# A Hymba layer on one core: last down-projection chunk reads pre-split operands, and orders change on DVE, GpSimd and in LayerNorm

## The chip, the cores and the metric

One core of a Trainium2 chip runs the whole layer. The metric is the device time of one execution in microseconds (us). The kernel before was run three times; the profile is of one more execution.

## The reference, cut to what matters

```python
h = layer_norm(x)                                   # 2048 tokens x 1024, float32
z = h @ w_in
y = concat(s5(z...), gla(z...), rg_lru(z...))       # three mixers
mix = y @ w_out                                     # 1024 x 1024
h = layer_norm(alpha * h + mix)                     # LN1
ff = square(relu(h @ mlp_w1)) @ mlp_w2              # 1024 -> 4096 -> 1024
h = layer_norm(alpha * h + ff)                      # LN2, the output
```

All is float32. The change touches the output projection with LN1, the two products of the MLP, and LN2.

## The kernel before, in words

**Number format.** A float32 product is made of three matmuls in a reduced format (`mm3`, L226 to L228): each operand is split into a high part (an ACT copy, L1373) and a low part (a subtraction on DVE of two tiles in SBUF); the matmuls take high x high, high x low and low x high. Names in the trace are those of tiles; L75 stands for every operation of DVE or GpSimd (POOL), since a helper records them, and L82 for every DMA, all issued from SP's queue.

**Winograd form.** Both MLP products use the seven-product form of a 2x2 block product (Strassen-Winograd). Operands are sums and differences of blocks; results come from sums of the products p1 to p7. The order of the products is p1, p2, p7, p6, p3 of the group before, p4, p5. Three kinds of PSUM banks hold them: bank a (3 buffers) p1, p6, p5, p3 added up; bank b (2) p2; bank c (2) p7 and p4. Each product is evacuated one slot after it is computed.

**Stages.** (1) Up to about 672 us: input projection and mixers. (2) 672 to 846: output projection. For each of 16 row tiles of 128 tokens the sum alpha*h + mix stays in SBUF (`acc`); LN1 runs on it (`ln1_work`, L1291, one generator that takes the rows one after another); `tj_work` (L1308) then takes two rows, transposes four 128x128 blocks at a time on TensorE (L1320, into `tjp`), copies them by ACT (L1324, L1325) into `tjo` and forms the Winograd sums there with two DVE and two POOL operations; a DMA stores them to `rop_d`. `tjo` has two buffers. (3) 846 to 958: the last of that work (`tail`) beside the first products of the MLP. The left operands of the up-projection are read back from `rop_d` into `ring` tiles and split (`ring_load`, `ring_split`); operand 6, which only p3 uses, comes last. (4) To 1541: 32 steps (`Step`), 16 column blocks for each half of the tokens, 84 matmuls each (19.0 us). A step splits its weight operands `w1o`; `Step.evac` and `hsum` make the hidden blocks c11, c21, c12, c22 (squared ReLU included) and their sums s1 to s4 in `cp` tiles, and `keep` stores the seven that the next product needs to `hid_d`, 256 KB each. (5) To 1594: entry into the down-projection. The first chunk of `mlp_w2` (tile `w`) is loaded, summed on POOL and split. (6) 1594 to 2103: chunks of the down-projection (`Chunk`), two column blocks of the hidden layer each, with 8 groups (`Part`, 42 matmuls, 9.5 us) per chunk. A part loads its operands `ho_m` from `hid_d` in 8 DMAs, splits them (three splits of 128x512, one of 128x256), and `Part.evac` adds seven products into `accq` (the rows of the output), some on DVE straight from PSUM, some on POOL from ACT's copies `p_m`, `u_m`. (7) From 2103: the eighth and last chunk. Here each group's two row tiles are final after it, and LN2 follows: `Acc.ln` (L1736: statistics on DVE, a power on POOL, a last operation on DVE) and `ln_apply` (L1754: ACT scales and shifts, L1756; DVE multiplies by the gain, 128x1024; POOL and DVE add the bias, 128x512 each; two stores).

**What sets the order.** Each engine works through its instructions in program order. `run` goes through the products; a table filled by `task(n, fn)` says which other work is written at which slot (one slot per product), so the numbers in those calls are the order of DVE, ACT, POOL and SP around the products:

```python
for g in range(8):
    n = M0 + 7 * (56 + g)
    for i, k in ((0, 13), (1, 14)):
        task(n + k, acc[g].ln, i)
        task(n + k + 2 + i, acc[g].ln_apply, i)
```

Of the kernel before, what the change touches and what calls it, by code (L numbers as in the profile page):

```python
# [40 lines left out]
def hymba_layer_kernel(  # L41
# [87 lines left out]
    hid_d = dram.tile([2, 16, 7, P, BLK], F32, name="hid_d")  # L129

# [1137 lines left out]
    def out_tile(i, dh):  # L1268
# [10 lines left out]
        def ev():  # L1279
            r = accs[i][:, dh * BLK:dh * BLK + BLK]  # L1280
            V.scalar_tensor_tensor(r, r, ALPHA, box["ps"], op0=ALU.mult, op1=ALU.add)
            if dh:
                z["acc", i] = True
# [4 lines left out]
    def ln1_work():  # L1288
        for i in range(NT):
            while ("acc", i) not in z:  # L1290
                yield  # L1291
            g = ln_steps(accs[i], z["gb1"], f"ln1_{i}", 384)
            next(g)
            yield
            yield
            yield
            for _ in g:
                yield
            late.append(bind(lambda i: store(h1_d[i * P:i * P + P, :], accs[i]), i))
            yield  # L1300
            z["row", i] = True
# [6 lines left out]
    def tj_work():  # L1308
        for i in range(2 * NT):
# [3 lines left out]
            if j == 0:  # L1313
                yield
# [17 lines left out]
            if j == 3:  # L1332
                late.append(bind(z.__setitem__, ("tj", g), True))
            yield
# [79 lines left out]
    def run(groups, tasks):  # L1414
# [25 lines left out]
        for g in groups:  # L1440
            for p in ORDER:
                who = prev if p == "p3" else g
                if who is not None:
                    products(who, p)
                evac()
                if who is not None:
                    last = who, p
# [42 lines left out]
    class Step:  # L1490
# [41 lines left out]
        def keep(self, i, nm):  # L1532
            store(hid_d[self.sb, self.c, i], self.out[nm])
# [45 lines left out]

    steps = [Step(n) for n in range(32)]  # L1580
# [24 lines left out]
    def tail():  # L1605
# [9 lines left out]
        for _ in range(4):  # L1615
# [12 lines left out]
    for n in range(11):  # L1628
# [8 lines left out]
    for n in range(31):  # L1637
# [25 lines left out]
    class Chunk:  # L1663
        def __init__(self, c):
            self.c = c
            self.op = [None] * 7

        def load(self):
            self.b = {}
            for j in range(2):  # L1670
                r = raw_tile([P, 2, D], f"w2_{self.c}_{j}")
                k = 4 * self.c + 2 * j
                load(r, w2_v[:, k:k + 2, :])
                self.b.update({("11", j): r[:, 0, 0:512], ("12", j): r[:, 0, 512:D],
                               ("21", j): r[:, 1, 0:512], ("22", j): r[:, 1, 512:D]})
# [458 lines left out]
```

## Time and profile before

| what | us |
|---|---|
| three runs | 2255.2, 2258.49, 2260.07 (median 2258.49) |
| the profiled execution | 2259.39 |
| its span in the trace | 2257.7 |
| PE busy in the span | 2067.0 (92%) |
| DVE, ACT, POOL busy | 1584.5, 1027.0, 1147.3 |
| DMA | 145 GB/s over the span |

PE is TensorE's matmul stream, PEld its weight loads, DVE the vector engine, ACT the scalar engine, POOL GpSimd, SP the engine whose queue issues the DMAs. A timeline row gives start, duration, engine, line, operation and tiles, and in brackets the engine's idle time before it with what ended it. PEclk is the granted share of TensorE's clock. The execution is 1.7 us longer than the span.

### The profile page before, as it was taken

Reading aid. Unit: us, or ns where it says so; the run is one execution under the profiler, and the core shown is the slowest. Engines: PE = TensorE matmul, PEld = TensorE weight load, DVE = VectorE, ACT = ScalarE, POOL = GpSimd, SP = SyncE. Lnnn points to the kernel's source line nnn. Section 1 sums busy time; section 2 is a strip of 40 time slices with the busy share of each in tenths; the row PEclk is TensorE's granted clock in tenths of the full one; section 3 lists DMA queues with packets and bytes.
Section 4 is the critical chain, followed back from the end, with each engine's and each line's share of the span. In section 5 each row is a group of like instructions: output and inputs, shape, how many; then the busy total and the mean of one; then the engine's idle time right before and its main releaser. Section 6 shows DMA issues by size and latency. Waiting matters only on the chain. (4 is left out here: it accounts for less than half of the span.)

```text
span 2257.7 us, 29781 instructions
## 1 busy us (share of the span) xinstructions
PE 2067.0 (92%) x9920; PEld 1712.9 (76%) x9920; DVE 1584.5 (70%) x2262; ACT 1027.0 (45%) x2045; POOL 1147.3 (51%) x1087
## 2 busy tenths in 40 slices
PE   6977999899999998799999999998999999999863
PEld 6866779888987776588887888886788888888652
DVE  6567865546547556677778877776688888888887
ACT  3336655657663222333334433334544545444431
POOL 5486630000003444466666666666566675667554
PEclk9998999999999999899999999999999999999976
DMA  7342354455354676544447444437544344434332
GB/s 212 102 129 74 98 167 137 121 138 140 99 177 131 175 232 204 146 150 153 150 154 256 151 153 154 148 128 266 185 131 135 94 134 131 135 98 134 111 105 77
DMA packets 378457, 328.24 MB, mean 145 GB/s; under 512 B 72240, under 2 KB 314560, under 8 KB 378304
## 3 DMA queue, kind: packets, MB, share of 16 engines
q1 hardware_dynamic: 377536, 324.24, 46.5%
q0 software_dynamic: 768, 2.11, 0.4%
q8 instruction: 78, 1.28, 0.2%
q14 instruction: 75, 0.61, 0.1%
HBM read 208.23 MB, written 118.63 MB: 145 GB/s over the span
## 5 line engine op out<-in xcount | busy, mean ns | idle before, releaser
L75 DVE TENSOR_TENSOR ho_m<-ho_m 128x512 fp32r<-128x512 f32 (+1 forms) x256 | 259.3, 1038 | 68.2 <-ACT ho_m L1373 55.9
L75 POOL TENSOR_TENSOR accq<-accq,p_m 128x512 f32<-128x512 f32 x128 | 199.9, 1579 | 200.4 <-DVE accq L75 155.9
L75 POOL TENSOR_TENSOR cp<-cp,cp 128x512 f32<-128x512 f32 x128 | 196.0, 1540 | 183.2 <-ACT cp L1562 180.6
L75 DVE TENSOR_TENSOR w1o_s<-w_s,w1o_s 128x512 fp32r<-128x512 f32 x160 | 208.6, 1318 | 46.6 <-ACT w1o_s L1373 46.5
L75 POOL TENSOR_TENSOR ss<-ss,cst 128x4 f32<-128x4 f32 x16 | 17.6, 1102 | 365.8 <-DVE ss L75 365.8
L227 PE MATMUL pa_m<-act,ho_m 128*128 128x512 f32 x384 | 150.4, 392 | 2.0 <-DVE act L75 1.9
L226 PE MATMUL pa_m<-act,ho_m 128*128 128x512 f32 x384 | 150.3, 391 | 2.0 <-ACT p_m L1792 1.4
L228 PE MATMUL pa_m<-act,ho_m 128*128 128x512 f32 x384 | 150.1, 391 | 1.2 <-DVE ho_m L75 1.2
L1373 ACT ACTIVATE ho_m<-ho_m 128x512 fp32r<-128x512 f32 (+1 forms) x256 | 135.6, 569 | 30.7 <-DMA ho_m<-hid_d 30.7
L1373 ACT ACTIVATE w1o_s<-w_s 128x512 fp32r<-128x512 f32 x160 | 99.9, 626 | 103.1 <-PE pb_s L228 51.8
L1792 ACT ACTIVATE p_m<-pa_m 128x512 f32<-128x512 f32 x64 | 38.3, 599 | 221.7 <-PE pa_m L228 216.0
L226 PE MATMUL pa_s<-ring,w1o_s 128*128 128x512 f32 x256 | 103.0, 402 | 11.0 <-ACT ring L1373 6.3
L226 PE MATMUL pc_m<-act,ho_m 128*128 128x512 f32 x256 | 102.4, 400 | 5.5 <-ACT p_m L1792 5.4
L226 PE MATMUL po<-act,w_mx 128*128 128x512 f32 x256 | 106.9, 418 | 0.1
L75 POOL TENSOR_TENSOR accq<-accq,u_m 128x512 f32<-128x512 f32 x64 | 106.2, 1659 | 0.6 <-ACT u_m L1792 0.6
L75 DVE SCALAR_TENSOR_TENSOR cp<-cp 128x512 f32<-128x512 f32 x96 | 101.9, 1061 | 3.3
L227 PE MATMUL pa_s<-ring,w1o_s 128*128 128x512 f32 x256 | 102.2, 399 | 1.9 <-DVE ring L75 1.9
L228 PE MATMUL po<-act,w_mx 128*128 128x512 f32 x256 | 103.2, 403 | 0.9 <-DVE w_mx L75 0.9
L227 PE MATMUL pc_s<-act,w1o_s 128*128 128x512 f32 x256 | 101.4, 396 | 1.8 <-DVE act L75 1.8
L227 PE MATMUL po<-act,w_mx 128*128 128x512 f32 x256 | 102.8, 402 | 0.0
L226 PE MATMUL pc_s<-act,w1o_s 128*128 128x512 f32 x256 | 102.6, 401 | 0.0
L228 PE MATMUL pc_m<-act,ho_m 128*128 128x512 f32 x256 | 101.5, 397 | 0.5 <-DVE ho_m L75 0.5
(437 smaller groups left out, 6553.3 us busy)
## 6 DMA issues: line engine op xcount, KB each, us to landing
hid_d<-cp SPq DMA_DIRECT2D x224, 256.0 KB, 2.3
ho_m<-hid_d SPq DMA_DIRECT2D x384, 128.0 KB, 2.3
w_s<-in_mlp_w_dram SPq DMA_DIRECT2D x32, 1024.0 KB, 5.7
w<-in_mlp_w_dram SPq DMA_DIRECT2D x16, 1024.0 KB, 7.0
rop_d<-tjo SPq DMA_DIRECT2D x32, 448.0 KB, 4.6
w<-s5w_d SPq DMA_DIRECT2D x16, 640.0 KB, 5.1
xr<-in_x_dram SPq DMA_DIRECT2D x16, 512.0 KB, 4.9
h_d<-xr SPq DMA_DIRECT2D x16, 512.0 KB, 4.4
```

The costliest lines, as they stand in the source:

```text
L75: return fn(*a, **k)
L226: T.matmul(ps, lhs[0], rhs[0], start=first, stop=False, skip_group_check=more)
L227: T.matmul(ps, lhs[0], rhs[1], start=False, stop=False, skip_group_check=more)
L228: T.matmul(ps, lhs[1], rhs[0], start=False, stop=last, skip_group_check=more)
L1373: S.activation(dst_hi, src, COPY)
L1792: S.activation(t, ps, COPY)
```

## The change

1. **Last chunk.** The chunks' column blocks are drawn from a table `CHUNK`; the last chunk takes blocks 3 and 11. Steps 3, 11, 19 and 27 make these; they no longer `keep` their seven tiles (28 stores fewer) but pass each through `parts`: an ACT copy into `hx` (2 buffers), a DVE subtraction in place, two stores to `hidx_d` (28 copies, 28 subtractions, 56 stores more). In the last chunk `Part.load` reads high and low parts with 16 DMAs in place of 8, and `split` does nothing.
2. **Part.evac.** For c21 and c22 DVE's add from PSUM is written before POOL's add of `u2` or `p7`.
3. **LN2.** Row tile 1 of a group is normalised at slots 10 and 12, row tile 0 at 13 and 15.
4. **LN1.** Each row has its own generator, started when its sum is complete; `tj_work` yields once more per four transposes; the tail goes over 18 slots in place of 11, with 6 yields before operand 6 is split.
5. **p3 of step 0** is computed at p7 of step 2 (before: in step 1); step 0's sums and step 2's operand 6 follow later.
6. **First chunk.** Its two weight tiles are loaded five slots before the last step and at it, and each is summed by itself.

```diff
                 last[0].evac(last[1])
             last = None
 
-        for g in groups:
+        for at_, g in enumerate(groups):
             for p in ORDER:
-                who = prev if p == "p3" else g
-                if who is not None:
-                    products(who, p)
-                evac()
-                if who is not None:
-                    last = who, p
+                if p != "p3":
+                    who = [(g, p)]
+                    if at_ == 2 and p == "p7":
+                        who.insert(0, (groups[0], "p3"))
+                else:
+                    who = [(groups[at_ - 1], p)] if at_ > 1 else []
+                for w in who:
+                    products(*w)
+                    evac()
+                    last = w
+                if not who:
+                    evac()
                 for e in tasks.pop(n, ()):
                     e()
                 n += 1
...
         def keep(self, i, nm):
-            store(hid_d[self.sb, self.c, i], self.out[nm])
+            if self.c not in CHUNK[-1]:
+                store(hid_d[self.sb, self.c, i], self.out[nm])
+
+        def parts(self, i, nm):
+
+            hi = z["sump"].tile([P, BLK], F32R, tag="hx", name=f"hx_{self.nm}_{i}", bufs=2)
+            raw = self.out[nm]
+            split(hi, raw.bitcast(F32R), raw)
+            for j, t in enumerate((f(hi), raw)):
+                store(hidx_d[self.sb, CHUNK[-1].index(self.c), i, j], t)
...
+    CHUNK = ((0, 1), (2, 4), (5, 6), (7, 8), (9, 10), (12, 13), (14, 15), (3, 11))
...
-        for _ in range(4):
+        for _ in range(6):
             yield
         for hf in range(2):
             ring_split(0, 6, hf)
...
-    for n in range(11):
+    for n in range(18):
...
-        for i, k in ((2, 2), (3, 3), (4, 4), (5, 6), (6, 6)):
+        for i, k in ((2, 2), (3, 3), (4, 4), (5, 6), (6, 11 if n == 1 else 6)):
             task(b + max(k, o), m.split, i)
     for n in range(32):
         s = 7 * n + 7
-        for w, k in ((1, 5), (3, 6), (2, 6), (4, 7)):
+        for w, k in ((1, 10), (3, 10), (2, 11), (4, 11)) if n == 0 else ((1, 5), (3, 6), (2, 6), (4, 7)):
             task(s + k, steps[n].hsum, w)
+        if steps[n].c in CHUNK[-1]:
+            for i, nm, k in ((0, "c11", 6), (4, "c22", 7), (2, "s3", 7), (5, "s1", 8), (1, "c21", 8), (3, "s2", 9),
+                             (6, "s4", 9)):
+                task(s + k, steps[n].parts, i, nm)
...
             for j in range(2):
-                load(f(t[:, 1, :, j, :]), hid_d[sb, 2 * self.ch.c + j, ops, :, tk].rearrange("o p c -> p o c"))
+                if self.ch.c < 7:
+                    load(f(t[:, 1, :, j, :]), hid_d[sb, CHUNK[self.ch.c][j], ops, :, tk].rearrange("o p c -> p o c"))
+                    continue
+                for h in range(2):
+                    load(f(t[:, h, :, j, :]), hidx_d[sb, j, ops, h, :, tk].rearrange("o p c -> p o c"))
...
-            split(t[:, 0], t[:, 1], f(t[:, 1]))
+            if self.ch.c < 7:
+                split(t[:, 0], t[:, 1], f(t[:, 1]))
...
             elif p == "p7":
-                self.add("c22", G, self.copy(bank["c"], "p7"))
+                self.p7 = self.copy(bank["c"], "p7")
             elif p == "p6":
-                self.add("c21", G, self.copy(bank["a"], "u2"))
+                self.u2 = self.copy(bank["a"], "u2")
             elif p == "p4":
                 self.add("c21", V, bank["c"])
+                self.add("c21", G, self.u2)
             elif p == "p5":
                 self.add("c22", V, bank["a"])
+                self.add("c22", G, self.p7)
...
-    task(L0, chunks[0].load)
-    for k, w in ((2, 3), (3, 1), (4, 2), (6, 4)):
+    task(L0 - 5, chunks[0].load, 0)
+    task(L0, chunks[0].load, 1)
+    for k, w, j in ((0, 3, 0), (1, 1, 0), (2, 3, 1), (3, 1, 1)):
+        task(L0 + k, chunks[0].sum, w, (j,))
+    for k, w in ((4, 2), (6, 4)):
         task(L0 + k, chunks[0].sum, w)
...
     for g in range(8):
         n = M0 + 7 * (56 + g)
-        for i, k in ((0, 13), (1, 14)):
+        for i, k in ((1, 10), (0, 13)):
             task(n + k, acc[g].ln, i)
-            task(n + k + 2 + i, acc[g].ln_apply, i)
+            task(n + k + 2, acc[g].ln_apply, i)
```

In `ln1_work` the outer loop over the rows and the wait for the row's sum are gone, and `active.append(ln1_work(i))` stands where the sum is complete; in `tj_work` a second `yield` stands at the end of the loop, and a wait for the first of the two rows ahead.

**DVE in the last chunk, one group.** Names are tiles of group 62, with LN2 of group 61 (`accq_5`); `gb2` holds gain and bias. Before:

```order
L75 TENSOR_TENSOR accq_6_0_13577<-accq_6_0_13577,pb_m62_18683 128x512
L75 TENSOR_TENSOR ho_m62_3_18644<-ho_m62_3_18644 128x256
L75 TENSOR_TENSOR ho_m63_1_18634<-ho_m63_1_18634 128x512
L75 TENSOR_TENSOR accq_4_1_13519<-accq_4_1_13519,gb2_18163 128x1024
L75 TENSOR_TENSOR accq_4_1_13519<-accq_4_1_13519,gb2_18163 128x512
L75 TENSOR_TENSOR ho_m63_2_18654<-ho_m63_2_18654 128x512
L75 TENSOR_TENSOR accq_5_0_13542<-accq_5_0_13542,pa_m61_18558 128x512
L75 TENSOR_TENSOR accq_6_1_13578<-accq_6_1_13578,pc_m62_18700 128x512
L75 BN_STATS st2_5_0_18756<-accq_5_0_13542 128x6 x2
L75 BN_AGGR mv2_5_0_18759<-st2_5_0_18756 128x2
L75 TENSOR_SCALAR rs2_5_0_18761<-mv2_5_0_18759 128x1
L75 SCALAR_TENSOR_TENSOR rs2_5_0_18761<-mv2_5_0_18759,rs2_5_0_18761 128x1
```

After:

```order
L75 TENSOR_TENSOR accq_6_0_13689<-accq_6_0_13689,pb_m62_18810 128x512
L75 BN_STATS st2_5_1_18842<-accq_5_1_13656 128x6 x2
L75 BN_AGGR mv2_5_1_18845<-st2_5_1_18842 128x2
L75 TENSOR_SCALAR rs2_5_1_18847<-mv2_5_1_18845 128x1
L75 SCALAR_TENSOR_TENSOR rs2_5_1_18847<-mv2_5_1_18845,rs2_5_1_18847 128x1
L75 TENSOR_TENSOR accq_5_0_13655<-accq_5_0_13655,pa_m61_18693 128x512
L75 TENSOR_TENSOR accq_5_1_13656<-accq_5_1_13656,gb2_18282 128x1024
L75 TENSOR_TENSOR accq_5_1_13656<-accq_5_1_13656,gb2_18282 128x512
L75 TENSOR_TENSOR accq_6_1_13690<-accq_6_1_13690,pc_m62_18825 128x512
L75 BN_STATS st2_5_0_18885<-accq_5_0_13655 128x6 x2
L75 BN_AGGR mv2_5_0_18888<-st2_5_0_18885 128x2
L75 TENSOR_SCALAR rs2_5_0_18890<-mv2_5_0_18888 128x1
```

The splits `ho_m` are gone. The statistics of row 1 stand in the first half of the group and those of row 0 in the second, and row 1's multiplication by the gain stands between them, ahead of the add of `pc_m`.

**ACT at the passage into the MLP.** `tjo_31` is the last transposed tile, `ring_0_6` operand 6 of the left side, `w1o_s2` the weight operands of step 2, `cp<-pa_s0` the evacuation of p3 of step 0. Before:

```order
L1324 ACTIVATE tjo_31_8775<-tjp_31_8747 128x256
L1325 ACTIVATE tjo_31_8775<-tjp_31_8747 128x128
L1373 ACTIVATE w1o_s2_1_8794<-w1_s2_8686 128x512
L1373 ACTIVATE w1o_s2_2_8814<-w1_s2_8686 128x512
L1537 ACTIVATE p7_s1_8829<-pc_s1_8797 128x512
L1373 ACTIVATE ring_0_6_0_8788<-ring_0_6_0_8788 128x2x512
L1373 ACTIVATE ring_0_6_1_8789<-ring_0_6_1_8789 128x2x512
L1373 ACTIVATE w1o_s2_3_8835<-s2_s2_8792 128x512
L1537 ACTIVATE u2_s1_8850<-pa_s1_8722 128x512
L1373 ACTIVATE w1o_s2_4_8852<-w1_s2_8686 128x512
L1561 ACTIVATE cp_4_8867<-pa_s0_8485 128x512
```

After:

```order
L1324 ACTIVATE tjo_31_8820<-tjp_31_8815 128x256
L1325 ACTIVATE tjo_31_8820<-tjp_31_8815 128x128
L1374 ACTIVATE w1o_s2_4_8828<-w1_s2_8669 128x512
L1374 ACTIVATE w1o_s2_5_8868<-s1_s2_8722 128x512
L1374 ACTIVATE w1o_s3_0_8890<-w1_s3_8728 128x512
L1553 ACTIVATE p1_s2_8908<-pa_s2_8871 128x512
L1374 ACTIVATE ring_0_6_0_8848<-ring_0_6_0_8848 128x2x512
L1374 ACTIVATE ring_0_6_1_8849<-ring_0_6_1_8849 128x2x512
L1374 ACTIVATE w1o_s3_1_8916<-w1_s3_8728 128x512
L1577 ACTIVATE cp_6_8931<-pa_s0_8490 128x512
```

The split of operand 6 and the evacuation of p3 of step 0 now stand behind p1 of step 2.

**DVE while step 5 runs, behind step 3.** `cp<-cp,hx` are the new subtractions for step 3's tiles. After:

```order
L75 TENSOR_TENSOR w1o_s5_6_9321<-w1_s5_9066,w1o_s5_6_9321 128x512
L75 TENSOR_TENSOR cp_16_9068<-cp_16_9068,hx_s3_0_9327 128x512
L75 TENSOR_TENSOR cp_28_9325<-pa_s4_9186,p7_s4_9265 128x512
L75 SCALAR_TENSOR_TENSOR cp_28_9325<-cp_28_9325 128x512
L75 TENSOR_TENSOR w1o_s6_0_9351<-w1_s6_9208,w1o_s6_0_9351 128x512
L75 TENSOR_TENSOR cp_22_9199<-cp_22_9199,hx_s3_4_9358 128x512
L75 TENSOR_TENSOR cp_24_9245<-cp_24_9245,hx_s3_2_9363 128x512
L75 TENSOR_TENSOR w1o_s6_1_9385<-w1_s6_9208,w1o_s6_1_9385 128x512
L75 TENSOR_TENSOR cp_26_9301<-cp_26_9301,hx_s3_5_9388 128x512
L75 TENSOR_TENSOR cp_20_9173<-cp_20_9173,hx_s3_1_9393 128x512
L75 TENSOR_TENSOR cp_30_9356<-pb_s5_9368,p1_s5_9381 128x512
L75 SCALAR_TENSOR_TENSOR cp_30_9356<-cp_30_9356 128x512
```

Before, the same rows stand without the `cp<-cp,hx`; the last two of the seven follow a row further on.

## Rows read from the trace of the kernel before

**Rows 1.** Busy time of each engine by stage (start:end, length; last PEclk, DMA share, GB/s).
```profile
672.00:846.50 174.50, 161.51 (x750) 130.74 (x749) 102.09 (x195) 52.47 (x137) 72.63 (x101) 0.96 0.61 184
846.50:958.30 111.80, 86.67 (x351) 68.67 (x350) 73.63 (x106) 36.39 (x70) 54.67 (x61) 0.86 0.57 174
1541.20:1594.00 52.80, 39.13 (x148) 28.95 (x149) 38.58 (x41) 27.58 (x46) 36.63 (x25) 0.94 0.83 282
1594.00:2103.00 509.00, 506.24 (x2226) 416.92 (x2225) 417.81 (x514) 249.37 (x475) 325.60 (x213) 1.00 0.41 123
2103.00:2257.70 154.70, 91.84 (x341) 71.42 (x339) 125.37 (x185) 47.79 (x71) 75.62 (x57) 0.78 0.31 98
```

**Rows 2.** TensorE's waits in the last chunk: total us, times, longest.
```profile
PE pa_m L226 <- DVE accq L75: 39.3, 7, 9.7
```

**Rows 3.** DVE's instructions by shape, one group, 2158.8 to 2176.55.
```profile
L75 DVE TENSOR_TENSOR ho_m<-ho_m 128x512 fp32r<-128x512 f32 x3 | 4.3, 1419 | 0.0
...
L75 DVE TENSOR_TENSOR ho_m<-ho_m 128x256 fp32r<-128x256 f32 x1 | 0.9, 907 | 0.0
L75 DVE TENSOR_TENSOR accq<-accq,pc_m 128x512 f32<-128x512 f32 x1 | 0.7, 686 | 0.6 <-POOL accq L75 0.6
```

**Rows 4.** Timeline of the same group.
```profile
2158.54 2.53 SPq L82 DMA_DIRECT2D ho_m<-hid_d  x5
...
2159.45 1.28 DVE L75 BATCH_NORM_STATS2 st<-accq 128x6 f32<-128x512 f32 x2
...
2162.08 1.24 ACT L1756 ACTIVATE accq<-accq,rs 128x1024 f32<-128x1024 f32 x1 [6.18 <-DVE rs L75]
...
2165.71 1.94 DVE L75 TENSOR_TENSOR accq<-accq,gb 128x1024 f32<-128x1024 f32 x2
...
2170.71 3.04 DVE L75 TENSOR_TENSOR accq<-accq,gb 128x1024 f32<-128x1024 f32 x2
```

**Rows 5.** Timeline, start and end of the last chunk.
```profile
2108.59 0.50 PE L226 MATMUL pa_m<-w2o,ho_m 128*128 128x512 f32 x1 [0.45 <-DVE accq L75]
...
2220.25 0.68 DVE L75 TENSOR_TENSOR accq<-accq,pb_m 128x512 f32<-128x512 f32 x1
...
2234.85 0.69 DVE L75 TENSOR_TENSOR accq<-accq,pa_m 128x512 f32<-128x512 f32 x1 [3.02 <-PE pa_m L228]
...
2252.01 1.76 POOL L75 TENSOR_TENSOR accq<-accq,gb 128x512 f32<-128x512 f32 x1 [1.17 <-DVE accq L75]
```

**Rows 6.** Timeline of TensorE in the group of rows 3.
```profile
2162.69 0.80 PE L226 MATMUL pa_m<-w2o,ho_m 128*128 128x512 f32 x1 [6.39 <-DVE accq L75]
...
2168.77 0.39 PE L228 MATMUL pa_m<-act,ho_m 128*128 128x512 f32 x1
```

**Rows 7.** Timeline of the passage into the MLP, TensorE and ACT.
```profile
912.45 0.63 ACT L1373 ACTIVATE w1o_s<-w_s 128x512 fp32r<-128x512 f32 x1 [5.15 <-POOL w_s L75]
...
917.09 0.45 PE L1320 MATMUL tjp<-ident,acc 128*128 128x128 f32 x1 [8.90 <-DVE tjo L75]
...
944.51 0.80 PE L226 MATMUL pa_s<-ring,w1o_s 128*128 128x512 f32 x1 [6.30 <-ACT ring L1373]
```

**Rows 8.** DMA issues: KB each, us from issue to landing.
```profile
hid_d<-cp SPq DMA_DIRECT2D x224, 256.0 KB, 2.3
...
rop_d<-tjo SPq DMA_DIRECT2D x32, 448.0 KB, 4.6
```

**Rows 9.** TensorE's waits in the output projection, 672 to 846.5.
```profile
PE tjp L1320 <- DVE tjo L75: 11.6, 6, 3.9
```

**Rows 10.** Timeline of the entry into the down-projection.
```profile
1533.86 1.29 POOL L75 TENSOR_TENSOR t<-w 128x512 f32<-128x512 f32 x1 [8.00 <-DMA w<-in_mlp_w_dram]
...
1588.96 0.79 PE L226 MATMUL pc_m<-act,ho_m 128*128 128x512 f32 x1 [5.39 <-ACT p_m L1792]
```

**Rows 11.** Busy time of each engine in one step, 1030.5 to 1049.5.
```profile
1030.50:1049.50 19.00, 19.00 (x85) 15.65 (x84) 13.85 (x13) 6.85 (x13) 12.62 (x8) 1.00 0.45 153
```

**Rows 12.** DVE's splits of the weights in that step.
```profile
L75 DVE TENSOR_TENSOR w1o_s<-w_s,w1o_s 128x512 fp32r<-128x512 f32 x5 | 6.6, 1343 | 1.6 <-ACT w1o_s L1373 1.6
```

More of the change, by code (lines that the diff above doesn't have):

```diff
@@ L129, in hymba_layer_kernel @@
     hid_d = dram.tile([2, 16, 7, P, BLK], F32, name="hid_d")
+    hidx_d = dram.tile([2, 2, 7, 2, P, BLK], F32, name="hidx_d")
     act = actp.tile([P, 2, KD, 2, BLK], F32R, name="act")
@@ L1282, in ev @@
             if dh:
-                z["acc", i] = True
+                active.append(ln1_work(i))
         for h in range(2):
@@ L1286, in out_tile, with ln1_work @@
             tick([un], bind(pe, h, un), ev if h else None)
[L1288 to L1293, printed above, removed]
-            yield
[L1295 to L1301, printed above, removed]
+    def ln1_work(i):
+        g = ln_steps(accs[i], z["gb1"], f"ln1_{i}", 384)
+        next(g)
+        yield
+        yield
+        yield
+        for _ in g:
+            yield
+        late.append(bind(lambda i: store(h1_d[i * P:i * P + P, :], accs[i]), i))
+        z["row", i] = True
     def set_gb(key, g_ap, b_ap, nm):
@@ L1313, in tj_work @@
             if j == 0:
+                while ("row", 2 * g) not in z:
+                    yield
                 yield
@@ L1333, in tj_work @@
                 late.append(bind(z.__setitem__, ("tj", g), True))
+            yield
             yield
@@ L1665, in __init__, with load, sum @@
             self.c = c
[L1666 to L1675, printed above, removed]
-        def sum(self, which):
+            self.op, self.b = [None] * 7, {}
+        def load(self, j):
+            r = raw_tile([P, 2, D], f"w2_{self.c}_{j}")
+            k = 2 * CHUNK[self.c][j]
+            load(r, w2_v[:, k:k + 2, :])
+            self.b.update({("11", j): r[:, 0, 0:512], ("12", j): r[:, 0, 512:D],
+                           ("21", j): r[:, 1, 0:512], ("22", j): r[:, 1, 512:D]})
+        def sum(self, which, js=(0, 1)):
             b = self.b
-            for j in range(2):
+            for j in js:
                 if which in (2, 3):
@@ L1850, in hymba_layer_kernel @@
             task(b + 6, chunks[c].split, 6)
-        task(b + 9, ch.load)
+        for j in range(2):
+            task(b + 9, ch.load, j)
         for k, w in ((15, 3), (22, 1), (33, 2), (40, 4)):
@@ L2034, in hymba_layer_kernel @@
                 z["tj bank"] = lambda i, shp, nm: psum("tp", shp, nm)
-                active.append(ln1_work())
                 active.append(tj_work())
```

## The prediction

> **What bounds the kernel now.** I read busy time by stage first. From 1594 to 2103 TensorE is busy 506.24 of 509 us: 0.2274 us for each of 2226 matmuls, at a granted clock of 1.00 [rows 1]. Nothing off TensorE can shorten that. Four other stretches have idle TensorE: the output projection (161.51 of 174.5), the passage into the MLP (86.67 of 111.8), the entry into the down-projection (39.13 of 52.8) and the last chunk (91.84 of 154.7, clock 0.78, DVE busy 125.37). Only there can the change gain. In the last chunk TensorE's waits name DVE's adds to `accq` seven times, 39.3 us, once per group [rows 2]: DVE sets that pace. The lines of one group show on what DVE spends its 17.75 us, and the timeline of the group gives the latencies of LN2 [rows 3, 4]. For the passage I followed TensorE's two longest waits back to what released them [rows 7]. A change between runs that is under 0.2% (4.5 us) I take as not to be told from none.
>
> **1. Last chunk: -30 us.** Removed from each DVE period: three subtractions, 4.3 us, and one of 0.9; as each instruction starts some 0.08 before the one ahead ends, 4.85 in all; and the wait of 0.6 for POOL [rows 3], since DVE's add from PSUM now stands first. If nothing new opened, the period would be 17.75 - 4.85 - 0.6 = 12.3. But the removed work lay in DVE's gaps while ACT applied LN2, so I walk the new order. An add costs 0.6 (0.686 less the overlap). Of one LN half, ACT starts 2.63 after the first statistics (2159.45 to 2162.08) and takes 1.24 [rows 4]; DVE is through with its scalars just before ACT starts, and I take 2.5 for it. In each half of the period: add 0.6, LN half 2.5, add 0.6 (beside ACT), a wait for the rest of ACT 0.8, then multiply and bias add 1.75 (the row of 1.94 less overlap). Two halves make 12.5. POOL's adds (now behind DVE's) meet one multiply, as in the row of 3.04 where the row without is 1.94 [rows 4]: I take 0.6 for it, half of that 1.1, and 0.25 for a power on POOL that comes behind an add. The period is 13.4. Ends: 12.3, and 15.5 (both multiplies held up by 1.1 and all else late by 0.8).
>
> Where it starts: p3 of group 55 starts at 2108.59 after 0.45 of wait [rows 5]; group 56 began four products of 1.36 (6 x 0.2274) ahead of that, at 2102.7. Nine products later (p1, p2, p7, p6 of 56, p3 of 55, p4, p5 of 56, p1, p2 of 57: 12.3) the add of p2 of group 57 can run: 2115.0. Six periods later the same add of group 63 runs, at 2115.0 + 6 x 13.4 = 2195.4; before it ran at 2220.25 [rows 5]. From there to POOL's last add: before 2252.01 + 1.76 - 2220.25 = 33.5. After, by the same prices: 10.0 to the add of p5 of 63, the wait of 3.0 for p3, which stays [rows 5], and its add 0.7; 1.75 for the gain of row 0 of group 62; LN2 of the two rows of group 63 one behind the other, each 2.5, then 1.4 for ACT's pass, then 1.75 in the first and 1.15 (the multiply alone) in the second; the last POOL add 1.8; 0.2 for an operation held up by POOL: 28.2. From POOL's end the span takes 3.9 more (2253.8 to 2257.7). New end 2227.5, **-30.2**; with the ends of the period -36.8 and -17.6.
>
> Its loads double: 16 DMAs per part in place of 8. Five of them take 2.53 of SP's queue [rows 4], 0.51 each, so 16 and the four stores take 10.1 of 13.4, and the DMA share is 0.31 [rows 1]. I charge nothing; the cover is 3.3 us in each period, and gone at a period of 10.
>
> TensorE's part: after 6.39 of idle the first matmul of the group takes 0.80, then 14 start within 6.08 (0.434 each) until they take 0.39 [rows 6]. That is the lower clock, 1.2 GHz, then 2.4 GHz. A group of 42 costs 14 x 0.434 + 28 x 0.2274 = 12.4, just under 13.4, so I keep DVE as the bound. The Trainium skill ("TensorE: Matmul & The Clock Gate", Part 1: The HAM clock gate) says that the throttled clock is the default and that activity releases it; the fall after the wait and the later rise agree. By the rows the last chunk gains 30; if every matmul stayed at the lower clock it is a rival, below.
>
> **2. Passage into the MLP: -15 us.** TensorE waited 8.90 at 917.09 for `tjo` and 6.30 at 944.51 for the ring's operand 6. The first came because ACT stood at a weight split behind a POOL sum until 912.45, with the copy of `tjp` behind it [rows 7]. After, `tjo` is asked for one to two products later (5.4 us each), so that wait shrinks to about 5, and p3 of step 0 stands behind p1 and p2 of step 2: two products of 2.7 fill what was the wait of 6.30. Stores of `rop_d` land after 4.6 [rows 8] and `tjo` has two buffers, so the last tile, its store, the ring's load and split cannot move earlier by more than a few us: I estimate that the split ends at 947.6, near where it does now, and p3 of step 0 at 949. All is then done that was done at 958.3, the stage's end, before, and two products more: 958.3 - 949 + 5.4 = **-14.7**. Ends: -25 (all idle gone, 111.8 - 86.67 [rows 1]) and -4 (the wait of 6.30 goes, and 2 come back in the later slots).
>
> **3. Output projection: -8 us.** TensorE's transposes wait 11.6 for `tjo` in six waits [rows 9]. One more yield puts a block of the projection's matmuls (12 x 0.2274 = 2.7) between them; LN1 rows no longer queue. Two thirds gone: **-8**; ends -13 (with all small idle) and +3 (the work lands in the tail).
>
> **4. Entry: -5 us.** POOL waited 8.00 for the weights at 1533.86; the last wait, 5.39, follows ACT behind a hidden operand's load while the DMA share is 0.83 [rows 1, 10]. Half the weights five slots earlier brings the sums forward by 2 to 3 us and their splits with them. Of 52.8 - 39.13 = 13.7 idle I take **-5**; ends -13.7 and +2, since the early load shares the DMAs with the hidden stores.
>
> **5. The four steps with `parts`: +1 us.** Seven subtractions of two SBUF tiles more, at 1.343 as the splits there [rows 12], are 9.4 per step; DVE has 19.0 - 13.85 = 5.15 free [rows 11]. The 4.3 left over run into the next step, which has its own 5.15. Some 3 us of stall behind hsums come on top; four product slots (10.8 us) lie between a late add and the bank's next use. So TensorE should not wait: **+1**, ends 0 and +8 (2 each). ACT has 12 us free and POOL 6 [rows 11]; 28 stores removed and 56 added are hidden behind a DMA share of 0.45.
>
> **Sum.** -30.2 - 14.7 - 8 - 5 + 1 = -57. The profiled execution was 2259.4, so 2202.5; the median shown is 0.9 below it: **2202**.
>
> **Rivals.**
> (A) *TensorE's clock becomes the bound of the last chunk.* If all 42 matmuls of a group run at the lower clock, they take 42 x 0.434 = 18.2, more than 17.75, and the period does not shrink; only the tail and start give 2 to 5. For: the clock of 0.78 and the row of 0.80. Against: waits become shorter than 6.39. About 2230. Chance 0.12.
> (B) *The chains of the passage and projection are paced by stores, not by order.* `rop_d` lands after 4.6 and two buffers serve 32 tiles; idle time goes from one wait into the next. Then parts 2 to 4 give -4, 0 and -3: 2259.4 - 30.2 - 7 + 1 = 2223. For: [rows 8]. Against: 912.45, where an ACT instruction was the cause. Chance 0.20.
> (C) *Slower: the tiles of `parts` go one behind another.* `hx` has two buffers; if each tile's copy (0.63 [rows 7]), subtraction 1.34 and store's landing 2.3 [rows 8] follow in series, seven take 29.9 per step, 24.7 more than DVE's 5.15, in four steps 99: 2202 + 99 - 1 = 2300. That is the one case that ends slower. It loses from (57/4 + 5.15)/7 = 2.8 us per tile on. Against: DVE itself waits only for the copy, and the two buffers let landings overlap. Chance 0.04.
> (D) *All covers work*: period 12.3 (-36.8), parts 2 to 4 near their best (-20, -12, -13), part 5 at 0: -82, so 2176. For: nothing in the order of DVE stands ahead of the adds that free TensorE. Against: each of these chains has a second wait behind the first. Chance 0.14.
>
> **How the numbers follow.** My forecast has 0.50, with 2190 to 2215 from the period's ends and half the spread of parts 2 to 4. The range takes in (A) and (B), and leaves out (C) and most of (D): 2180 to 2232. All bounds at their worst still give -17.6 - 4 + 3 + 2 + 8 = -8.6, faster by 0.4%. So faster 0.95, the same 0.01, slower 0.04 (C).
>
> **What would show it.** Right: in the last chunk the `pb_m` adds of DVE stand 13 to 14 apart, no `ho_m` subtraction appears, TensorE waits there about 1 us per group; one wait of about 5 near 912 and none at 944; DVE in steps 4 and 5 over 18 of 19 busy with TensorE at 19.0. Wrong: periods over 16 with a clock under 0.6 (A); transposes that wait for DMA (B); a step of over 25 us after steps 3, 11, 19, 27 (C).

## The result, and the profile after

| | before | after |
|---|---|---|
| median of four runs | 2257.84 | 2219.43 |
| range | 2255.2 to 2260.07 | 2217.24 to 2223.48 |
| the profiled execution, its span | 2259.39, 2257.7 | 2217.24, 2215.5 |

The ratio is 0.9832 (95% interval 0.9814 to 0.9851): 1.7% faster, 38 us by the medians and 42.2 by the two spans. 2202 was forecast, with 2180 to 2232 as the range. The time lies in the range, but a term of the sum is far off, and others make up for part of it. The kernel after was run four times, and so were e1_wload, e5_nosplit, e9_best and e13_best3 below; the other experiments were run once.

To see which, I cut both spans at the same points of the work: the first matmul of the output projection; the first matmul of product p2 in step 5, in step 31, in group 4 of the first down-projection chunk and in group 56 (the first of the last chunk); and the end. Busy time of each engine by these stretches, before (start:end, length; PE, PEld, DVE, ACT, POOL busy; PEclk, DMA share, GB/s):

```profile
654.92:1018.35 363.43, 323.02 (x1437) 261.52 (x1435) 229.39 (x361) 121.07 (x266) 166.82 (x187) 0.93 0.57 179
1018.35:1526.46 508.11, 502.30 (x2185) 411.62 (x2184) 377.46 (x352) 194.35 (x325) 332.39 (x209) 0.99 0.47 161
1526.46:1604.06 77.60, 63.03 (x254) 48.27 (x252) 49.48 (x56) 38.09 (x64) 47.36 (x32) 0.96 0.82 276
1604.06:2103.90 499.84, 497.08 (x2185) 409.43 (x2184) 412.64 (x506) 242.89 (x464) 319.85 (x208) 1.00 0.41 122
2103.90:2257.70 153.80, 90.94 (x337) 70.67 (x335) 124.47 (x184) 47.79 (x71) 75.43 (x56) 0.78 0.31 98
```

and after:

```profile
655.23:984.41 329.18, 307.01 (x1436) 251.32 (x1435) 232.66 (x360) 122.50 (x268) 167.77 (x187) 0.98 0.62 194
984.41:1519.97 535.56, 512.12 (x2186) 417.96 (x2184) 388.75 (x381) 207.63 (x351) 328.30 (x210) 0.97 0.50 171
1519.97:1595.31 75.34, 63.12 (x253) 48.41 (x252) 52.48 (x57) 38.02 (x64) 46.33 (x31) 0.95 0.81 271
1595.31:2092.95 497.64, 497.23 (x2185) 409.38 (x2184) 436.33 (x509) 239.27 (x461) 300.60 (x208) 1.00 0.42 125
2092.95:2215.50 122.55, 86.06 (x337) 67.38 (x335) 84.37 (x149) 34.25 (x42) 69.56 (x58) 0.85 0.57 172
```

Lengths subtracted, beside the forecast:

| stretch | forecast | measured |
|---|---|---|
| projection and passage (parts 2, 3) | -22.7 | -34.3 |
| steps 5 to 30, all four with `parts` behind them (part 5) | +1 | **+27.4** |
| entry (part 4) | -5 | -2.3 |
| chunks 1 to 7 | 0 | -2.2 |
| last chunk (part 1) | -30.2 | -31.3 |

The steps are where the expected time stayed. In them TensorE is busy 23 us less than the stretch lasts, where before it was 6; the other 10 of the 27 us are matmuls that take longer, 512.1 us in place of 502.3 at a granted clock of 0.97 in place of 0.99. TensorE's waits in three stretches after (total, times, longest): the projection up to 865.5, the passage and steps from 958 to 1540, the last chunk; the first answers to [rows 9], the last to [rows 2]:

```profile
PE tjp L1320 <- DVE tjo L75: 0.8, 1, 0.8
...
PE pc_s L228 <- ACT p_s L1553: 17.5, 4, 4.5
...
PE pa_m L228 <- DVE accq L75: 17.4, 6, 7.1
```

The projection's six waits of 11.6 are one of 0.8, and the last chunk's 39.3 are 17.4. The middle row is new: four times, about 4.4 us each, TensorE waits for ACT's copy `p_s`. The timeline around the first of them, behind step 3 (SPq rows are DMAs issued):

```profile
986.03 0.62 ACT L1374 ACTIVATE w1o_s<-w_s 128x512 fp32r<-128x512 f32 x1
...
987.13 0.39 SPq L82 DMA_DIRECT2D w_s<-in_mlp_w_dram  x1
987.61 0.66 SPq L82 DMA_DIRECT2D hidx_d<-hx_s  x1
...
994.21 0.63 ACT L1374 ACTIVATE hx_s<-cp 128x512 fp32r<-128x512 f32 x1 [7.56 <-DMA hidx_d<-hx_s]
...
999.34 0.58 ACT L1553 ACTIVATE p_s<-pc_s 128x512 f32<-128x512 f32 x1
...
999.97 0.50 PE L228 MATMUL pc_s<-act,w1o_s 128*128 128x512 f32 x1 [4.44 <-ACT p_s L1553]
```

and the DMAs issued from 987.0 to 988.2, with the time to landing:

```profile
w_s<-in_mlp_w_dram SPq DMA_DIRECT2D x1, 1024.0 KB, 6.4
...
hidx_d<-hx_s SPq DMA_DIRECT2D x1, 256.0 KB, 6.5
```

To be read from below: TensorE's p4 needs the bank that ACT's copy of p7 frees (999.34). That copy stands on ACT behind copies into `hx`, and the first of these waited 7.56 us for a store of `hx` to land. The store was issued 0.48 behind a weight load of 1 MB and landed after 6.5 us, where a 256 KB store took 2.3 in the trace of before [rows 8]. The same happened after steps 11, 19 and 27: the four steps in which it happens last 25.5 to 26.3 us from p2 to p2, those around them 19.2. After the wait the clock is low too; the ten us behind it:

```profile
999.90:1009.95 10.05, 9.98 (x37) 8.03 (x37) 6.90 (x9) 4.45 (x9) 5.90 (x5) 0.83 0.55 203
```

37 matmuls take 9.98, where 37 x 0.2274 is 8.4: 4.4 of wait and 1.6 of clock make 6.0 of the 6.4 that this step lost.

### The profile page after: what moved, and what is told of

It reads as the page before. It is cut to its first block, busy times and chain, and to the rows that moved or that the text cites. A ratio compares the mean times of both kernels' runs of the same rounds, so it can differ in the third digit from the quotient of the medians.

```text
span 2215.5 us, 29837 instructions
## 1 busy us (share of the span) xinstructions
PE 2056.8 (93%) x9920; PEld 1704.5 (77%) x9920; DVE 1585.7 (72%) x2258; ACT 1024.4 (46%) x2041; POOL 1116.6 (50%) x1087
## 4 chain that ended last, share of the span: by engine, by line
PE 43%; DVE 5%; ACT 3%; DMA 3%; POOL 3%; issue 2%; SPq 0%; POOLq 0%; DVEq 0%; ACTq 0%
PE pa_s L229 4%; PE pa_s L230 4%; PE pa_s L228 4%; PE pa_m L228 4%; PE pa_m L230 4%; PE pa_m L229 4%; PE pc_s L228 2%; PE pc_s L230 2%; PE pc_s L229 2%; POOL accq L75 2%; PE pc_m L228 2%; PE pc_m L229 2%; PE pc_m L230 2%; DMA hidx_d<-hx_s 2%; DVE accq L75 1%
## 5 line engine op out<-in xcount | busy, mean ns | idle before, releaser
L75 DVE TENSOR_TENSOR ho_m<-ho_m 128x256 fp32r<-128x256 f32 (+1 forms) x224 | 249.7, 1145 | 59.8 <-ACT ho_m L1374 37.4
L75 DVE TENSOR_TENSOR w1o_s<-w_s,w1o_s 128x512 fp32r<-128x512 f32 x160 | 193.0, 1217 | 41.6 <-ACT w1o_s L1374 41.5
L75 POOL TENSOR_TENSOR accq<-accq,p_m 128x512 f32<-128x512 f32 x128 | 182.0, 1429 | 68.1 <-DVE accq L75 60.2
L75 POOL TENSOR_TENSOR accq<-accq,u_m 128x512 f32<-128x512 f32 x64 | 87.3, 1364 | 159.4 <-DVE accq L75 137.8
L1374 ACT ACTIVATE ho_m<-ho_m 128x256 fp32r<-128x256 f32 (+1 forms) x224 | 117.8, 570 | 15.8 <-DMA ho_m<-hid_d 15.6
L228 PE MATMUL pc_s<-act,w1o_s 128*128 128x512 f32 x256 | 106.6, 416 | 17.5 <-ACT p_s L1553 17.5
L228 PE MATMUL pc_m<-act,ho_m 128*128 128x512 f32 x256 | 102.2, 399 | 6.2 <-ACT p_m L1817 5.8
L229 PE MATMUL pc_s<-act,w1o_s 128*128 128x512 f32 x256 | 104.5, 408 | 2.1 <-DVE act L75 2.1
L230 PE MATMUL pc_s<-act,w1o_s 128*128 128x512 f32 x256 | 104.8, 409 | 0.0
L228 PE MATMUL po<-act,w_mx 128*128 128x512 f32 x256 | 103.3, 404 | 0.0
L230 PE MATMUL po<-act,w_mx 128*128 128x512 f32 x256 | 100.2, 392 | 1.4 <-DVE w_mx L75 1.4
L75 DVE TENSOR_TENSOR accq<-accq,pa_m 128x512 f32<-128x512 f32 x128 | 86.9, 679 | 20.4 <-PE pa_m L230 20.4
```

The costliest lines, as they stand in the source:

```text
L75: return fn(*a, **k)
L228: T.matmul(ps, lhs[0], rhs[0], start=first, stop=False, skip_group_check=more)
L229: T.matmul(ps, lhs[0], rhs[1], start=False, stop=False, skip_group_check=more)
L230: T.matmul(ps, lhs[1], rhs[0], start=False, stop=last, skip_group_check=more)
L1374: S.activation(dst_hi, src, COPY)
```

## The experiments

All twelve, cut at the same points, as the change of each stretch against before (spans of the profiled executions; each kernel is the changed one with one edit, unless said otherwise). The table is worked out from the starts of matmuls in the timelines.

| run | projection, passage | steps | entry | chunks | last chunk | span |
|---|---|---|---|---|---|---|
| the change | -34.3 | +27.4 | -2.3 | -2.2 | -31.3 | 2215.5 |
| e1_wload | -34.0 | +5.8 | -3.1 | -2.2 | -31.3 | 2192.8 |
| e2_nosub | -30.8 | +18.2 | -2.0 | -2.2 | -31.3 | 2210.9 |
| e12_hx3 | -33.0 | +16.7 | +0.1 | -2.3 | -31.3 | 2210.1 |
| e5_nosplit | -30.3 | 0.0 | -1.1 | -2.2 | -12.7 | 2213.6 |
| e3_evac | -33.5 | +27.8 | -2.7 | +0.1 | -18.3 | 2232.6 |
| e4_ln2 | -33.9 | +27.4 | -2.0 | -2.3 | -32.3 | 2215.9 |
| e6_yield | -20.4 | +27.7 | -1.9 | -2.3 | -31.3 | 2229.9 |
| e7_serial | -23.7 | +27.9 | -1.4 | -2.3 | -31.4 | 2226.2 |
| e11_p3 | -9.7 | +27.5 | -1.6 | -2.2 | -31.3 | 2241.0 |
| e8_entry | -34.0 | +27.8 | +1.9 | -2.2 | -31.1 | 2219.8 |
| e9_best | -33.3 | +4.9 | -2.7 | -2.3 | -35.5 | 2190.4 |
| e13_best3 | -33.3 | +1.3 | -2.4 | -2.4 | -35.6 | 2186.1 |

Where an edit does not touch a stretch, it repeats within 0.5 us, but for the first (-30.3 to -34.3) and the entry (-3.1 to +0.1): differences there count only beyond that.

**The four steps.** Theory (the buffer theory below): `hx` has two buffers, a store lands late behind the weight load, and ACT's queue passes the wait on to TensorE. Rivals: DVE has no room for seven more subtractions; 56 more stores are too much for the queue.

e1_wload, the weight load four slots later in these steps:

```diff
-            task(max(5, b - 7), m.load)
+            task(max(5, b - 7) + (4 if n in (6, 14, 22, 30) else 0), m.load)
```

> The changed kernel, with the 1 MB weight load that falls into each of the four steps' splitting of tiles issued four slots later. Buffer theory: the high copies on ACT wait for a landing store because two buffers serve seven tiles and a store queued behind the 1 MB load lands late; the copy of p7 stands behind them on ACT and TensorE waits for its bank. Then the extra 6.4 to 7.1 us of each of the four steps shrinks to under 3, and the time falls by 16 to 27 us to about 2192 to 2203. DVE theory (seven more subtractions than DVE has room for) and volume theory (56 more stores on the queue): the four steps stay at 6 to 7 us each, no change.

Measured: median 2198.08, ratio to before 0.974 (0.9721 to 0.9759), the steps +5.8 in place of +27.4. DMAs and subtractions are as many as before the edit, so both rivals fall as the main cause. In its timeline behind step 3 the store that took 6.5 lands after 2.3 (issued 986.89), ACT waits 2.85 for it in place of 7.56, and the load comes behind the last `hx`:

```profile
989.26 0.63 ACT L1374 ACTIVATE hx_s<-cp 128x512 fp32r<-128x512 f32 x1 [2.85 <-DMA hidx_d<-hx_s]
...
998.06 0.50 PE L228 MATMUL pc_s<-act,w1o_s 128*128 128x512 f32 x1 [2.75 <-ACT p_s L1553]
...
998.69 0.40 SPq L82 DMA_DIRECT2D w_s<-in_mlp_w_dram  x1
```

What stays (2.75 here) is still ACT waiting, four times now, for landings between tiles; the other three steps lose about 1 us each.

e2_nosub, an ACT copy in place of the split, so that the low part is not formed:

```diff
-            split(hi, raw.bitcast(F32R), raw)
+            S.activation(hi, raw, AF.Copy)
```

> The changed kernel without the 28 subtractions in the four steps: the low parts are stored as whole values, which leaves the subtraction of the high part out. DVE theory: the four steps lose their extra 27 us in all, about 2192. Buffer theory: the copies still wait for landing stores, the four steps keep 5 us each or more, 2212 or higher.

Measured: span 2210.9, the steps +18.2. Between the two expectations: most of the loss stays without any subtraction, as the buffer theory has it, but 9 us go, and TensorE's four waits are 11.4 in place of 17.5. It is not DVE's time as such (e13_best3, below, keeps all 28 subtractions). The traces point to the order on SP: behind step 3 the second tile's high part is stored 5.2 us after its copy started in the change (982.39, 987.61) and 3.5 after in this run (986.81, 990.31), since on SP it stands behind a store of a tile that DVE makes after a subtraction. How much of the 9 us this accounts for no run separates.

e12_hx3, a third buffer:

```diff
-        ur = smallp.tile([P, 256], F32, tag="u_row", name=f"ur_{b}_{t}", bufs=2)
+        ur = const.tile([P, 256], F32, tag="u_row", name=f"ur_{b}_{t}", bufs=2)
...
-            hi = z["sump"].tile([P, BLK], F32R, tag="hx", name=f"hx_{self.nm}_{i}", bufs=2)
+            hi = z["sump"].tile([P, BLK], F32R, tag="hx", name=f"hx_{self.nm}_{i}", bufs=3)
...
-                                                       name=f"t{which}_{self.c}_{j}", bufs=2 if own else 1)
+                                                       name=f"t{which}_{self.c}_{j}", bufs=3 if own else 1)
```

(The last edit is for the weight sums of the down-projection, which use the same buffers later.)

> The changed kernel with three buffers for the high copies in place of two; a tile of the input stage (two rows of 1 KB) moves to another pool to make room, the weight load stays where it is. Buffer theory: a copy waits for the store before the one before last, so the four steps' 27.5 us shrink by a third or more, to 5 to 18. If only the weight load's place in the queue matters and not the number of buffers: 27 as before.

Measured: span 2210.1, the steps +16.7. A buffer more gives 11 us, as the theory asks. It does not cure the late landing: ACT's long wait is still 8.0 to 8.2 in each of the four steps, one tile later, and TensorE's four waits are 10.8 in place of 17.5.

**The last chunk.** e5_nosplit takes the early splitting out (`keep` stores always, no `parts`, `load` and `split` as for the other chunks):

```diff
-        if steps[n].c in CHUNK[-1]:
+        if False:
```

> The changed kernel without the splitting ahead of time: steps 3, 11, 19 and 27 store whole tiles, the last chunk splits its operands itself; everything else as in the changed kernel. If the split is what the last chunk gains from, its period goes from 13.2 back by 4.85 to about 18 (six periods, 25 to 29 us), and the four steps give back 27: within 5 us of 2219. Rival: the orders of POOL and LN2 alone give the last chunk its gain; then the period stays near 13 to 14 and the time is about 2192.

Measured: median 2211.01, ratio 0.9795 (0.9779 to 0.9812), 8 us faster than the change. The steps give back all 27.4, the last chunk loses 18.6, less than expected; the period (adds of p2 to `accq`) is 16.0, where the change has 13.27. So as written, the early splitting lost 9 us, and its cost in the steps hid its gain. Why 16.0 and not the 18 expected: the splits fall in part into time in which DVE would wait. Its waits for ACT in the last chunk are a third of the change's 11.2 (shown below):

```profile
DVE accq L75 <- ACT accq L1776: 4.0, 4, 1.3
```

e3_evac puts POOL's adds first again:

```diff
-                self.p7 = self.copy(bank["c"], "p7")
+                self.add("c22", G, self.copy(bank["c"], "p7"))
...
-                self.u2 = self.copy(bank["a"], "u2")
+                self.add("c21", G, self.copy(bank["a"], "u2"))
```

> The changed kernel with POOL's adds of u2 and p7 ahead of DVE's adds again. If DVE waited for POOL there, each group of the last chunk is longer by 0.5 to 1.5 us (4 to 10 in all), and the small gain of 0.4 us per chunk from 1594 to 2103 goes: about 2223 to 2230. Rival: the POOL adds are ready in time in the new order of LN2; no change.

Measured: span 2232.6; the last chunk 13.0 longer, more than expected, and the 2.2 of the chunks ahead go exactly. The period is 15.03. How: its timeline of POOL and DVE in one group,

```profile
2154.33 2.52 POOL L75 TENSOR_TENSOR accq<-accq,p_m 128x512 f32<-128x512 f32 x2
2156.81 0.55 POOL L75 TENSOR_TENSOR rs<-rs,cst 128x1 f32<-128x1 f32 x1
2157.33 1.29 POOL L75 TENSOR_TENSOR accq<-accq,u_m 128x512 f32<-128x512 f32 x1
...
2157.39 1.24 DVE L75 SCALAR_TENSOR_TENSOR rs<-mv,rs 128x1 f32<-128x1 f32 x1 [1.93 <-POOL rs L75]
```

and the same two engines in the change:

```profile
2158.36 1.28 POOL L75 TENSOR_TENSOR accq<-accq,p_m 128x512 f32<-128x512 f32 x1
2159.60 0.54 POOL L75 TENSOR_TENSOR rs<-rs,cst 128x1 f32<-128x1 f32 x1
...
2160.18 0.16 DVE L75 SCALAR_TENSOR_TENSOR rs<-mv,rs 128x1 f32<-128x1 f32 x1 [0.72 <-POOL rs L75]
```

With the old order two POOL adds (2.52) stand ahead of LN2's power, DVE waits 1.93 for it in place of 0.72, and then its own 128x1 operation takes 1.24 in place of 0.16, beside the third add. That is 1.21 + 1.08 more per group; 0.5 comes back, since DVE's two multiplies by the gain now run clear of POOL's adds (mean 1226 ns in place of 1485); the sum, 1.8, is the difference of the periods. DVE's waits for POOL's power in the last chunk, in this run and in the change:

```profile
DVE rs L75 <- POOL rs L75: 20.0, 16, 2.0
```

```profile
DVE rs L75 <- POOL rs L75: 11.2, 16, 0.7
DVE accq L75 <- ACT accq L1776: 11.2, 14, 1.3
```

This holds beside the new slots of LN2. In the kernel before, with the old order of both, it was DVE's adds that waited for POOL's, and the power cost no more than in the change:

```profile
DVE rs L75 <- POOL rs L75: 11.4, 16, 0.7
DVE accq L75 <- POOL accq L75: 8.2, 8, 3.1
```

What the order of `evac` is worth with LN2 in its old slots was not run.

e4_ln2 puts LN2 back into its slots:

```diff
-        for i, k in ((1, 10), (0, 13)):
+        for i, k in ((0, 13), (1, 14)):
...
-            task(n + k + 2, acc[g].ln_apply, i)
+            task(n + k + 2 + i, acc[g].ln_apply, i)
```

> The changed kernel with the slots of LN2 as before (both rows one behind the other at the end of the group). If the order matters because DVE waits for ACT's passes, the period of 13.2 grows by 1 to 2.5 us, 6 to 15 us in all, about 2225 to 2234. Rival: DVE's busy time alone sets the period; then no change.

Measured: 2217.59, span 2215.9, the last chunk 1 us shorter. Neither expectation as put: the old slots make the period shorter (12.7 from group 57 to 63), since one row's statistics run while ACT handles the other, and DVE no longer waits the 11.2 for ACT that the change shows (its waits for POOL's power stay, 11.4); the tail behind the last p2 add gives 2.0 of it back (33.9 after 31.9). With the other edits in place, the new order of LN2 gains nothing.

**The projection and the passage.** e6_yield takes out the second `yield` in `tj_work`:

```diff
             yield
-            yield
```

> The changed kernel without the additional yield per four transposes. If the spacing of the transposes is what removed their waits in the projection, 6 to 10 us of those waits come back before the last matmul of the projection. Rival: the rows' own LN1 generators made the transposes possible earlier, and the spacing adds nothing: the projection ends within 2 us of the changed kernel's.

Measured: span 2229.9; the last matmul of the projection comes 16.6 later than in the change, more than the range of 6 to 10. Of these, 11.7 are waits and 5.0 the longer time of as many matmuls. TensorE's longest waits in the projection (672 to 882), where the change has 0.8 for `tjo` and 2.0 for `acc`:

```profile
PE tjp L1320 <- DVE tjo L75: 7.9, 5, 2.3
PE po L228 <- ACT w_mx L1945: 3.1, 1, 3.1
PE tjp L1320 <- DVE acc L75: 3.1, 2, 1.7
```

e7_serial brings back one generator for LN1, the function as before:

```diff
-                active.append(ln1_work(i))
+                z["acc", i] = True
...
+                active.append(ln1_work())
                 active.append(tj_work())
```

> The changed kernel with LN1 again in one generator that takes the rows one after another. If the queue of rows was part of what held the transposes, the projection ends 3 to 12 us later than in the changed kernel and the last transpose with it. Rival: the spacing alone did it; within 2 us.

Measured: span 2226.2; counted from the projection's first matmul, its last comes 8.0 later and the last transpose 10.8 later. Both parts are needed; within the projection the spacing is worth more.

e11_p3 is e6_yield with `run`, the sums of step 0 and operand 6 as before:

```diff
-                    if at_ == 2 and p == "p7":
-                        who.insert(0, (groups[0], "p3"))
...
-        for _ in range(6):
+        for _ in range(4):
...
-        for w, k in ((1, 10), (3, 10), (2, 11), (4, 11)) if n == 0 else ((1, 5), (3, 6), (2, 6), (4, 7)):
+        for w, k in ((1, 5), (3, 6), (2, 6), (4, 7)):
```

> The run without the additional yield, and with p3 of step 0, its sums and operand 6 in the slots of before (the two cannot be undone in the other order, since operand 6 is split later in the changed kernel). Against the run without the yield: if the later p3 is what shortens the passage, the gain of 15.4 between the first MLP product and step 2 falls to 0 to 8, a wait of about 6 for the ring's operand 6 comes back. Rival: the rows' own generators did it; the passage stays as it is.

Measured: span 2241.0. From the first MLP product to p2 of step 5, behind all that was moved, the kernel before takes 125.6 us, e6_yield 110.4 and this run 121.0: the gain is 4.5 in place of 15.1. The wait for the ring is back at 6.7:

```profile
PE pa_s L228 <- ACT ring L1373: 6.7, 1, 6.7
```

So the later p3, with the sums and the split that moved along with it, is worth 10.6 us: 7.1 of waits, and 3.5 because as many matmuls take 103.8 in place of 107.2 (granted clock 0.95 and 0.91).

**The entry.** e8_entry:

```diff
-    task(L0 - 5, chunks[0].load, 0)
+    task(L0, chunks[0].load, 0)
...
-    for k, w, j in ((0, 3, 0), (1, 1, 0), (2, 3, 1), (3, 1, 1)):
+    for k, w, j in ((2, 3, 0), (2, 3, 1), (3, 1, 0), (3, 1, 1)):
```

> The changed kernel with both weight tiles of the first chunk loaded at the last step, and their sums two and three slots after, as before. If the early load is worth something, the entry (from the last step's start to the fourth group of the first chunk), now 2.3 us shorter than before, becomes 1 to 4 us longer. Rival: the waits of the entry come from the hidden operands; no change.

Measured: span 2219.8, the entry 4.1 longer than in the change and 1.9 longer than before. Little of this is waiting. The entry's busy time in this run, and in e12_hx3, which leaves the entry alone:

```profile
1520.08:1599.53 79.45, 66.49 (x254) 50.55 (x252) 51.23 (x57) 38.22 (x64) 46.16 (x31) 0.91 0.80 270
```

```profile
1512.27:1589.99 77.72, 66.75 (x253) 51.42 (x252) 51.29 (x57) 37.87 (x64) 46.47 (x31) 0.89 0.78 262
```

TensorE's idle time grows by 0.7 against the change (12.96 after 12.22); the other 3.4 are matmuls at a lower clock (66.49 after 63.12), and e12_hx3 has them too, with the load early. So what the early load is worth is not shown: 0.7 of waits, and of the clock perhaps nothing.

**A version that beats both.** e9_best is e1_wload with LN2 as in e4_ln2 and, at the end of `run`, the work of group 62 ahead of the last add of p3:

```diff
         products(prev, "p3")
+        for k in sorted(tasks):
+            if k < n + 4:
+                for e in tasks.pop(k):
+                    e()
         prev.evac("p3")
```

> The changed kernel with the later weight load of the first run of this study, LN2 in the slots of before, and the sums, gain and statistics of group 62 written ahead of the add of p3 of group 63, so that DVE has work while TensorE makes that product. Against the first run (2198): LN2's slots 1 us less, the wait of 3.0 filled, about 2194. If LN2's slots cost nothing only beside that wait, 2198.

Measured: median 2194.54, ratio 0.9719 (0.9702 to 0.9735); last chunk 4.2 shorter than the change's, as expected. e13_best3 is e9_best with the edits of e12_hx3:

> The kernel of the best run so far (later weight load, LN2 in the slots of before, work under the last p3; 2194.5) with three buffers for the high copies. Buffer theory: of the 5 us that the four steps still cost, most go: 2190 to 2193. DVE theory for that remainder: 2194 to 2195.

Measured: median 2188.36 (2186.51 to 2190.48), ratio 0.9688 (0.9672 to 0.9704), 31 us below the change. The steps cost 1.3 in all, with all 28 subtractions and 56 stores in them: neither DVE's time nor the number of stores is by itself the cause. Its waits for the copy of p7 from 940 to 1540 are one of 1.0:

```profile
PE pc_s L228 <- ACT p_s L1557: 1.0, 1, 1.0
```

## Why the prediction was right, and where not

**The last chunk (part 1), right in size.** The adds of p2 stand 13.27 apart (2104.03 for group 57, 2183.62 for group 63, six periods) against 13.4; from the last of them to the span's end it is 31.9 against 32.1. The lines of one group of the change, which answer to [rows 3]:

```profile
L75 DVE TENSOR_TENSOR accq<-accq,gb 128x1024 f32<-128x1024 f32 x2 | 3.0, 1486 | 1.4 <-ACT accq L1776 1.4
...
L75 DVE SCALAR_TENSOR_TENSOR rs<-mv,rs 128x1 f32<-128x1 f32 x2 | 0.3, 159 | 1.4 <-POOL rs L75 1.4
```

Of waiting for ACT there are 0.7 per half of the period, where the walk had 0.8; the 0.7 per half for POOL's power lie inside its 2.5 for an LN half. But the prices of the single edits ahead of the walk were off. The wait of 0.6 for POOL stood for the order of `evac`; taking that order back costs 1.8 per period (15.03 after 13.27, e3_evac), since beside the new slots of LN2 it is the power, not the add, that POOL's queue delays. The splits, set at 4.85 per period, are worth 2.7 (16.0 to 13.27), since in e5_nosplit they fill waits in part. The period came out because the walk goes through the order as it stands after the change and needs no price for a single edit. Of the signs named, the `pb_m` adds stand 13.2 to 13.4 apart as said; TensorE waits 1.8 to 2.8 per group there, not about 1.

**The four steps (part 5), wrong: this is the step that failed.** It said "So TensorE should not wait: +1, ends 0 and +8"; measured +27.4. It weighed DVE's busy time and gave ACT "12 us free". ACT was free, but it was held: it ran nothing for 7.56 us while the copy at its head waited for a buffer, the copy of p7 stood five instructions behind that one, and the buffer's store lay behind a 1 MB load. Nothing in part 5 priced a wait of ACT, and its sign of being right, TensorE at 19.0 in steps 4 and 5, did not come (25.5 in step 5). Rival (C) had the two buffers and the landing, and its sign came: each of the four steps lasts over 25 us. But it priced every tile alike at 4.3 with 2.3 for a landing; what happened was one long wait of ACT per step (7.56 to 8.05), and 1.0 us per tile on average (27.4 / 28), below the 2.8 from which (C) decides. Its words against, that the two buffers let landings overlap, did not hold: in e1_wload, with landings of 2.3 to 4.6 behind step 3, ACT still waits for one four times.

**Projection and passage (parts 2, 3), right in direction, too small:** -34.3 against -22.7. The waits in the projection shrank more than said ([rows 9], two thirds to go; now 0.8). What the sum did not have is the clock. Over the whole stretch, idle time of TensorE falls by 18.2 us and the time of its matmuls by 16.0 (323.0 to 307.0). Busy time up to the first MLP product, before and after:

```profile
672.00:892.80 220.80, 198.81 (x915) 160.99 (x913) 133.02 (x247) 65.24 (x162) 95.41 (x129) 0.96 0.61 186
```

```profile
672.30:871.20 198.90, 189.68 (x915) 155.66 (x913) 139.63 (x247) 65.53 (x163) 96.91 (x129) 1.00 0.69 207
```

As many matmuls, 915, take 198.8 at 0.96 and 189.7 at 1.00: 9.1 us, beside 12.8 less of idle time. In the passage the wait of 8.90 for `tjo` [rows 7] was to shrink to about 5, because `tjo` is asked for later. It is 8.09 (at 892.75), and its cause stayed: ACT again stands at a weight split behind a POOL sum, with the copies of `tjp` behind it:

```profile
889.42 0.63 ACT L1374 ACTIVATE w1o_s<-w_s 128x512 fp32r<-128x512 f32 x1 [6.00 <-POOL w_s L75]
```

The wait of 6.30 [rows 7] is gone as said, by the moved p3 (e11_p3); 0.71 is left at 928.42.

**Entry (part 4):** -2.3 against -5, inside its ends, but no more than the entry's scatter from run to run, and e8_entry does not show that the early load made it. **Chunks 1 to 7:** -2.2 where nothing was said; e3_evac shows that it is the order of `evac`.

**The sum, inside its range in part by luck.** Part 5 missed by 26.4 us and the entry by 2.7 on the slow side; projection, passage, chunks and last chunk missed by 14.9 on the fast side. With projection and passage as forecast, the median would be 2231, just under the upper end of 2232.

**The rivals.** (A) did not come: waits became shorter and TensorE's clock in the last chunk is 0.85 after 0.78. (B) did not: the projection's chain followed the order of work, and in the passage the wait that stayed comes from ACT's order (889.42), not from a store. (D) needed the period of 12.3; with LN2's old slots it is 12.7, and e13_best3 lies 12 us above the 2176 of (D).

## What to carry to other kernels

An engine with idle time is not a free place: ask of each instruction put on it what it waits for (a buffer, and with it the landing of a store, and what was issued ahead of that store), and who stands behind it in the queue. Price a periodic stretch by walking the whole order once, waits included; the prices of single edits were off here by nearly two one way (4.85 for 2.7) and three the other (0.6 for 1.8). A wait of TensorE can cost more than its length: 1.6 us of clock behind 4.4 of wait in a step, 9.1 beside 12.8 in the projection. So split a difference between runs into idle time and time of the matmuls before you credit it to a wait: in e8_entry most of it was clock.

## What the runs showed of the hardware that I had not expected

A store of 256 KB that was issued 0.48 us behind a load of 1 MB landed after 6.5 us, about when the load did (6.4); with the load issued four slots later the same store landed after 2.3, and 21.6 of 27.4 us went out of the steps (e1_wload). Whether the store waits its turn behind the load or shares the transfer with it, no run separates.

A DVE operation on 128x1 elements took 1.24 us where it takes 0.16: it started 0.06 after a POOL add of 1.29 and ended with it (e3_evac, 2157.39). The Trainium skill ("SBUF — State Buffer", Who interferes with whom, and Summary: rules for kernel authors) says that a DVE instruction with two inputs in SBUF contends with a GpSimd instruction that reads SBUF, and that the second one to issue is blocked until the first finishes. These two rows agree, and the smallest operation of a chain was the one that paid.
